# Order of three helpers' work in a macaron decoder kernel: the attention's levels, the normed blocks, the last norm's scale

## The chip, the cores and the metric

The kernel runs on one core of a Trainium2 chip. The metric is the device time of one launch in microseconds: 1767.38 us, the median of three runs (1766.87 to 1767.44). The engines are named as the profile does: PE (TensorE's matmuls; PEld its weight loads), DVE (VectorE), ACT (ScalarE), POOL (GpSimd) and SP (the queue that loads weights).

## The reference

Two layers of a decoder over 512 tokens of width 1024. The first mixes tokens by gated linear attention (4 heads), the second by stick-breaking attention (16 heads); each mixer stands between two half-step SwiGLU feed-forward blocks, and a last RMSNorm ends the trunk. All of it is in float32.

```python
def swiglu(h, w_gate, w_up, w_down):
    return (jax.nn.silu(h @ w_gate) * (h @ w_up)) @ w_down

for i in range(DEPTH):                     # DEPTH = 2
    x = x + 0.5 * swiglu(rmsnorm(x, ffn1_norm[i]), ...)
    h = rmsnorm(x, mix_norm[i])
    y = gla_mixer(h, ...) if i % 2 == 0 else sb_mixer(h, ...)
    x = x + y
    x = x + 0.5 * swiglu(rmsnorm(x, ffn2_norm[i]), ...)
return rmsnorm(x, final_norm)
```

Inside the linear attention, with `b` the running sum of the log decay of a chunk:

```python
o_inter = einsum('bhtk,bhkv->bhtv', q_t * exp(b_t), state)
scores  = einsum('bhtk,bhtsk,bhsk->bhts', q_t, exp(b_t - b_s) (causal), k_t)
o_intra = einsum('bhts,bhsv->bhtv', scores, v_t)
k_dec   = k_t * exp(b_last - b_t)
state   = exp(b_last) * state + einsum('bhsk,bhsv->bhkv', k_dec, v_t)
```

## The kernel before

The activations stay on the chip as eight tiles `x0` to `x7` of 128 features by 512 tokens. The kernel runs six phases one after the other: FFN1, the linear attention (GLA), FFN2, FFN3, the stick-breaking attention and FFN4. Weights come in from memory in chunks; each operand of a matmul is split into a high part, rounded to the matmul's short form (`wh` by a cast on ACT, L151), and a low part, what the rounding left (`wl` by a subtraction on DVE, L152). A product is then three matmuls (`mm3`): high by high, low weight by high, high weight by low. The activations are split in the same way (`nh` and `nl` for normed blocks, `xh` and `xl` for ones that are only scaled by the norm's weights, `sh` and `sl` for the summed squares). The feed is a list of entries, one weight tile each; starting an entry issues the casts of up to three entries ahead, and `wh` and `wl` have four buffers each.

The order on each engine is the program's order unless a scope changes it. `tc.high_priority(n)` lets what is issued inside it go ahead of other work that is ready; `ahead()` is that scope with a large n. `tc.issue_after(ins)` puts what is issued inside it behind one named instruction. Each engine then works through its list in order, and an instruction that waits holds up all that is behind it on its engine.

The places that matter here:

- `feat` (L217 on) multiplies all eight blocks of the activations (`st["h"]`, `st["l"]`) with one weight tile of 128 features. It takes the blocks in the order 0 to 7. In an FFN the first entries run on the scaled blocks, and the norm's root is applied after the matmul; meanwhile `normed_input` makes normed blocks (`xn` L878, `nh` L884, `nl` L885) in pairs: 0 and 4, 1 and 5, 2 and 6, 3 and 7. After that the entries use them, and only the scaled ones' results are still multiplied by the root `R`.
- `sums_wide` (L602 on) sums the squares over the features for FFN2, FFN3 and FFN4: it casts the sum `ss` (`sh`, ACT, L605), subtracts (`sl`, DVE, L607) and sends both through TensorE against ones, into `ps_R`. `rstd_wide` makes `R` of that on DVE and ACT (L617 to L625). `two_halves` interleaves two entries of the feed and calls `sums_wide` between them, to be issued behind the fourth-last matmul recorded so far.
- GLA works head by head. `levels` builds a chunk's causal scores by seven block sizes; for each, `prepare` makes a tile `e`: two subtractions of decays (L1168, L1169, DVE), an exponential on ACT, and two products with k and q (L1171, L1172, DVE). The score matmuls read `e` into a bank `ps_S`, and DVE picks each level's share out of it (L1187, L1211), which frees the bank. `output` makes the decayed keys `kd` (L1237, an exponential, L1244), transposes them on TensorE (`ps_kd`, L1255), updates the state (L1275, L1277) and norms the head's output (L1296 to L1321). `evac_q`, `evac_k`, `evac_v` and `evac_g` empty the matmul banks of q, k, v and the output gate (`gn`, L1070); the output gate then goes on with `sg` and `gn` (L1076, L1080). Between these steps the feed's matmuls run.
- `to_tokens` (L1632 on) turns the x tiles to token rows at the end of FFN4, after the last updates of x (L365). It loads the last norm's weights as `fin` and multiplies them by a constant on DVE (L1649), put behind the last of ACT's copies of the turned tiles; `last` reads `fin`.

Of the kernel before, what the change touches and what calls it, by code (L numbers as in the profile page):

```python
# [18 lines left out]
P = 128  # L19
# [27 lines left out]
def decoder(ctx: ExitStack, tc: tile.TileContext, a: dict, out: bass.AP):  # L47
# [284 lines left out]
    def down(w, r0, nf, hs, part, nxt, late=0, homes=()):  # L332
# [7 lines left out]
        def body(W):  # L340
# [13 lines left out]
            for m in range(nd):  # L354
# [3 lines left out]
                if m < len(homes):  # L358
# [242 lines left out]
    def sums_wide(pool, after):  # L601

        ss = st["ss"]
        h = sp.tile([P, T], F32R, tag="sq", name="sh")
        nc.scalar.copy(h, ss)  # L605
        l = pool.tile([P, T], F32R, tag="t", name="sl")
        nc.vector.tensor_tensor(out=l, in0=ss, in1=h.bitcast(F32), op=ALU.subtract)  # L607
# [19 lines left out]
    def two_halves(between=None):  # L627
# [28 lines left out]
    class FFN:  # L656
# [328 lines left out]
        def run(self, between=None):  # L985
            with tc.tile_pool(name="hp", bufs=8, reuse_waits="tile") as self.hp, tc.tile_pool(
# [34 lines left out]
    class GLA:  # L1021
# [25 lines left out]

        def evac_q(self, h, ps):
            self.q[h] = self.page("q")
            nc.vector.scalar_tensor_tensor(  # L1050
                out=pair(self.q[h]),
                in0=flat(ps),
                scalar=float(P) ** -0.5,
                in1=pair(st["R"]),
                op0=ALU.mult,
                op1=ALU.mult,
            )

        def evac_k(self, h, ps):
            self.k[h] = self.page("k")  # L1060
            nc.vector.tensor_tensor(out=pair(self.k[h]), in0=flat(ps), in1=pair(st["R"]), op=ALU.mult)

        def evac_v(self, c, i, ps):
            nc.scalar.activation(
                pair(self.v[i][:, c * 256 : c * 256 + 256]), flat(ps), AF.Copy, scale=st["r4"][:, i : i + 1]
            )

        def evac_g(self, j, ps):
            self.gn[j] = self.gp.tile([P, T], F32, tag="g", name="gn")
            nc.vector.tensor_tensor(out=pair(self.gn[j]), in0=flat(ps), in1=pair(st["R"]), op=ALU.mult)  # L1070
# [82 lines left out]
        def levels(self, h):  # L1153
# [6 lines left out]
            def prepare(B):  # L1160
# [10 lines left out]
                nc.vector.tensor_tensor(out=e0, in0=e0, in1=halves(k)[0], op=ALU.mult)  # L1171
                nc.vector.tensor_tensor(out=e1, in0=e1, in1=halves(q)[1], op=ALU.mult)  # L1172
                return e

            def seconds(t, B):
# [55 lines left out]
        def output(self, h):  # L1231
# [5 lines left out]
            nc.vector.tensor_tensor(  # L1237
                out=kd[:, 0:n3].rearrange("p (n s) -> p n s", n=3),
                in0=bl[:, 0:3].to_broadcast([P, 3, P]),
                in1=b[:, 0:n3].rearrange("p (n s) -> p n s", n=3),  # L1240
                op=ALU.subtract,
            )
            act(kd[:, 0:n3], kd[:, 0:n3], AF.Exp)
            nc.vector.tensor_tensor(out=kd[:, 0:n3], in0=kd[:, 0:n3], in1=k[:, 0:n3], op=ALU.mult)  # L1244
# [388 lines left out]
    def to_tokens(tp):  # L1633
# [3 lines left out]
        for hf in range(2):  # L1637
# [5 lines left out]
                    )  # L1643
            for i in range(NT):
                xt[i, hf] = xs[hf * 4 + i]
                copied = nc.scalar.copy(xt[i, hf], ps[i]).ins

        with tc.issue_after(copied):
            nc.vector.tensor_scalar(out=fin, in0=fin, scalar1=2.0 * float(D) ** 0.5, scalar2=None, op0=ALU.mult)  # L1649

    def last(dh, i, ps, c0, c1):
# [336 lines left out]
```

## Time and profile before

| what | value |
| --- | --- |
| median of three runs | 1767.38 us (1766.87 to 1767.44) |
| profiled execution | 1767.14 us, of which the span from first to last instruction is 1765.2 us |
| DVE busy | 1506.7 us (85%) |
| ACT busy | 1063.3 us (60%) |
| TensorE's granted clock | 0.999 |
| bytes read | 175.17 MB, 100 GB/s over the span |

In the rows below, a row of the timeline is: start and duration in microseconds, engine, line of the program, operation, output and inputs by the program's names, shapes, number of instructions; in brackets how long the engine was idle ahead of it and what ended that. A matmul's duration contains the time in which it overlaps with the next, so the pace of matmuls is read from one start to the next. The share of busy time is an average: TensorE is busy nearly all the time, and what an edit is worth is read from the places at which TensorE stands.

### The profile page before, as it was taken

The numbers are of one execution on the slowest core, as the hardware profiler recorded it, in microseconds if no ns is written. First come the engines' busy times: TensorE is split into PE (matmuls) and PEld (weight loads), VectorE is DVE, ScalarE is ACT, GpSimd is POOL, SyncE is SP. The second block draws the span as 40 slices with busy tenths as digits, with TensorE's granted clock in tenths as the row PEclk, the third lists the DMA queues.
The fourth block names the chain that finished last, engine by engine and source line by source line (L and its number), as shares of the span: only waits on it lengthen the run. The fifth ranks groups of instructions, "written<-read, shape, count | busy, mean of one in ns | idle before, by whom it ended". The sixth has DMA issues, their size and how long they took to land.

```text
span 1765.2 us, 31380 instructions
## 1 busy us (share of the span) xinstructions
PE 1751.6 (99%) x12714; PEld 1630.2 (92%) x12714; DVE 1506.7 (85%) x2490; ACT 1063.3 (60%) x1899; POOL 55.7 (3%) x77
## 2 busy tenths in 40 slices
PE   9999999999999999999999999999999999999998
PEld 8999999889888899999989999999888889999997
DVE  8999797786888999889799988977898679997986
ACT  7556555554655565555656555656888745555555
POOL 0000000200000000000000000010000000000000
PEclk9999999999999999999999999999999999999999
DMA  5543435422123433444434334352212234434341
GB/s 168 155 122 106 136 105 149 113 72 72 50 89 103 125 114 120 120 120 126 133 94 132 106 123 135 102 131 83 84 49 74 70 96 132 132 99 129 110 136 61
DMA packets 186389, 193.14 MB, mean 109 GB/s; under 512 B 4931, under 2 KB 171125, under 8 KB 186245
## 3 DMA queue, kind: packets, MB, share of 16 engines
q1 hardware_dynamic: 177760, 175.91, 31.9%
q0 software_dynamic: 8240, 14.95, 4.6%
q8 instruction: 99, 1.62, 0.4%
q14 instruction: 46, 0.37, 0.1%
q10 hardware_dynamic: 244, 0.29, 0.0%
HBM read 175.17 MB, written 2.10 MB: 100 GB/s over the span
## 4 chain that ended last, share of the span: by engine, by line
PE 86%; DVE 9%; ACT 3%; issue 1%; DMA 1%; SPq 0%; DVEq 0%; ACTq 0%
PE ps_w L776 22%; PE ps_d L80 15%; PE ps_q L776 11%; PE ps_f L80 10%; PE ps_z L776 5%; PE ps_w L410 5%; PE ps_t L80 4%; PE ps_b L80 3%; PE ps_q L410 2%; DVE wl L152 1%; PE ps_z L410 1%; PE ps_z L1476 1%; PE ps_oT L1561 1%; DVE xn L878 1%; PE ps_bt L80 1%
## 5 line engine op out<-in xcount | busy, mean ns | idle before, releaser
L152 DVE TENSOR_TENSOR wl<-raw,wh 128x1024 fp32r<-128x1024 f32 x241 | 255.1, 1059 | 40.7 <-ACT wh L151 40.0
L151 ACT CAST wh<-raw 128x1024 fp32r<-128x1024 f32 x241 | 222.2, 923 | 71.5 <-PE ps_f L80 25.4
L152 DVE TENSOR_TENSOR wl<-s,wh 128x1024 fp32r<-128x1024 f32 x160 | 195.2, 1220 | 64.5 <-ACT wh L151 64.0
L776 PE MATMUL ps_w<-th,wh 128*128 128x256 f32 x864 | 239.0, 277 | 0.2
L776 PE MATMUL ps_w<-th,wl 128*128 128x256 f32 x864 | 237.7, 275 | 1.2 <-DVE wl L152 1.2
L776 PE MATMUL ps_w<-tl,wh 128*128 128x256 f32 x864 | 237.6, 275 | 0.0
L151 ACT CAST wh<-s 128x1024 fp32r<-128x1024 f32 x160 | 168.6, 1054 | 6.0 <-DVE s L762 6.0
L776 PEld LDWEIGHTS ps_w<-th,wh 128*128 128x128 f32 x864 | 165.8, 192 | 1.4 <-ACT o L813 1.1
L776 PEld LDWEIGHTS ps_w<-th,wl 128*128 128x128 f32 x864 | 165.8, 192 | 1.4 <-DVE wl L152 1.4
L80 PE MATMUL ps_f<-xh,wh 128*128 128x512 f32 x432 | 166.4, 386 | 0.0
L776 PEld LDWEIGHTS ps_w<-tl,wh 128*128 128x128 f32 x864 | 165.9, 192 | 0.0
L80 PE MATMUL ps_f<-xh,wl 128*128 128x512 f32 x432 | 164.2, 380 | 0.5 <-DVE wl L152 0.5
L80 PE MATMUL ps_f<-xl,wh 128*128 128x512 f32 x432 | 163.9, 379 | 0.0
L80 PE MATMUL ps_d<-hh,wh 128*128 128x512 f32 x416 | 157.8, 379 | 0.0
L80 PE MATMUL ps_d<-hh,wl 128*128 128x512 f32 x416 | 157.7, 379 | 0.0
L80 PE MATMUL ps_d<-hl,wh 128*128 128x512 f32 x416 | 157.7, 379 | 0.0
L152 DVE TENSOR_TENSOR wl<-rawd,wh 128x1024 fp32r<-128x1024 f32 (+1 forms) x100 | 94.8, 961 | 8.0 <-ACT wh L151 8.0
L804 ACT COPY ps_z<-ps_w 128x256 f32<-128x256 f32 x72 | 26.0, 362 | 118.1 <-PE ps_w L776 117.9
L361 POOL DMA_DIRECT2D x<-d x53 | 46.0, 913 | 1555.0 <-ACT d L360 1097.4
L80 PEld LDWEIGHTS ps_f<-xl,wh 128*128 128x128 f32 x432 | 81.7, 189 | 11.6
L80 PEld LDWEIGHTS ps_f<-xh,wl 128*128 128x128 f32 x432 | 81.7, 189 | 11.4 <-DVE wl L152 0.9
L80 PEld LDWEIGHTS ps_f<-xh,wh 128*128 128x128 f32 x432 | 81.7, 189 | 10.8
(357 smaller groups left out, 5426.0 us busy)
## 6 DMA issues: line engine op xcount, KB each, us to landing
raw<-in_ffn_w_gate_dram SPq DMA_DIRECT2D x43, 1024.0 KB, 5.4
raw<-in_ffn_w_up_dram SPq DMA_DIRECT2D x43, 1024.0 KB, 5.4
rawd<-in_ffn_w_down_dram SPq DMA_DIRECT2D x84, 512.0 KB, 3.9
x<-d POOLq DMA_DIRECT2D x53, 256.0 KB, 4.6
raw<-in_gla_w_in_dram SPq DMA_DIRECT2D x12, 1024.0 KB, 5.3
raw<-in_sb_w_in_dram SPq DMA_DIRECT2D x16, 512.0 KB, 3.7
raw<-in_gla_w_out_dram SPq DMA_DIRECT2D x4, 1024.0 KB, 5.6
raw<-in_sb_w_in_dram SPq DMA_DIRECT2D x4, 1024.0 KB, 5.1
```

Of the source, the lines that this page charges most:

```text
L80: st["pe"] = nc.tensor.matmul(ps, l, r, start=first, stop=last).ins
L151: nc.scalar.copy(h[:, k], part)
L152: nc.vector.tensor_tensor(out=l[:, k], in0=part, in1=h[:, k].bitcast(F32), op=ALU.subtract)
L361: nc.gpsimd.dma_start(xs[k], d, accum_op=ALU.add)
L410: st["pe"] = nc.tensor.matmul(ps, l_, r_, start=first and c + n == 0, stop=c == 1 and n == 2, skip_group_check=True).ins
L776: st["pe"] = nc.tensor.matmul(o, l_, r_, start=first and j + n == 0, stop=j == 3 and n == 2, skip_group_check=True).ins
L804: v["copied"] = nc.scalar.copy(z, w).ins
L878: nc.vector.scalar_tensor_tensor(out=t, in0=xs[k], scalar=g, in1=st["R"], op0=ALU.mult, op1=ALU.mult)
L1476: nc.tensor.matmul(o_, l_, r_, start=first, stop=last, skip_group_check=True)
L1561: nc.tensor.matmul(po[e * 64 : e * 64 + 64, j * P : T], self.v[j][:, c : c + 64], self.wt[p, e][bk][:, c0 : c0 + n], start=j == 0, stop=j ...
```

## The change

Four edits; no instruction is added or removed, and the lists of POOL and SP stay as they are.

1. `feat` takes the blocks in the order `st["made"]`. That is 0 to 7 at a phase's start, and 0, 4, 1, 5, 2, 6, 3, 7 once the normed blocks are used.
2. `sums_wide` gets two instructions: the high part's matmul is issued behind the fourth-last matmul recorded, as before, the low part's behind the last one.
3. In GLA the evacuations of q, k, v and the gate, all of `prepare`, and `kd` are issued inside `ahead()`.
4. The last norm's scaling is issued behind the last update of x instead of behind ACT's last copy.

```diff
-                for k in part:
-                    mm3(ps, wh[:, k], wl[:, k], st["h"][k], st["l"][k], k == 0, k == KD - 1)
+                for i in part:
+                    k = st["made"][i]
+                    mm3(ps, wh[:, k], wl[:, k], st["h"][k], st["l"][k], i == 0, i == KD - 1)
...
-                nc.vector.scalar_tensor_tensor(
+                st["updated"] = nc.vector.scalar_tensor_tensor(
                     out=x, in0=flat(ps), scalar=0.5, in1=x, op0=ALU.mult, op1=ALU.add
-                )
+                ).ins
...
-        with tc.high_priority(100), tc.issue_after(after):
-            mm(ps, ones_r, turns(h), True, False)
-            mm(ps, ones_r, turns(l), False, True)
+        for r, ins, first in ((h, after[0], True), (l, after[1], False)):
+            with tc.high_priority(100), tc.issue_after(ins):
+                mm(ps, ones_r, turns(r), first, not first)
...
-                    between(recent[-4])
+                    between((recent[-4], recent[-1]))
...
-        st["h"], st["l"] = st["nh"], st["nl"]
+        st["h"], st["l"], st["made"] = st["nh"], st["nl"], range(KD)
...
                 st["h"], st["l"] = zip(*self.n)
+                st["made"] = [k for j in range(4) for k in (j, j + 4)]
...
         def evac_k(self, h, ps):
             self.k[h] = self.page("k")
-            nc.vector.tensor_tensor(out=pair(self.k[h]), in0=flat(ps), in1=pair(st["R"]), op=ALU.mult)
+            with ahead():
+                nc.vector.tensor_tensor(out=pair(self.k[h]), in0=flat(ps), in1=pair(st["R"]), op=ALU.mult)
...
-                nc.vector.tensor_tensor(out=e0, in0=ref, in1=b0, op=ALU.subtract)
-                nc.vector.tensor_tensor(out=e1, in0=b1, in1=ref, op=ALU.subtract)
-                act(e, e, AF.Exp)
-                nc.vector.tensor_tensor(out=e0, in0=e0, in1=halves(k)[0], op=ALU.mult)
-                nc.vector.tensor_tensor(out=e1, in0=e1, in1=halves(q)[1], op=ALU.mult)
+                with ahead():
+                    nc.vector.tensor_tensor(out=e0, in0=ref, in1=b0, op=ALU.subtract)
+                    nc.vector.tensor_tensor(out=e1, in0=b1, in1=ref, op=ALU.subtract)
+                    act(e, e, AF.Exp)
+                    nc.vector.tensor_tensor(out=e0, in0=e0, in1=halves(k)[0], op=ALU.mult)
+                    nc.vector.tensor_tensor(out=e1, in0=e1, in1=halves(q)[1], op=ALU.mult)
...
-                copied = nc.scalar.copy(xt[i, hf], ps[i]).ins
-
-        with tc.issue_after(copied):
+                nc.scalar.copy(xt[i, hf], ps[i])
+
+        with tc.issue_after(st["updated"]):
             nc.vector.tensor_scalar(out=fin, in0=fin, scalar1=2.0 * float(D) ** 0.5, scalar2=None, op0=ALU.mult)
```

`evac_q`, `evac_v`, the first operation of `evac_g` and the three operations of `kd` are put inside `ahead()` in the same way.

Three places show how the engines' lists change. The line numbers of the changed kernel are up to eight higher than those of the kernel before.

The first is DVE in FFN4, before, around the last norm's scaling:

```order
L365 SCALAR_TENSOR_TENSOR x_84<-ps_d,x_84 128x512
L1649 TENSOR_SCALAR fin<-fin 128x1024
L152 TENSOR_TENSOR wl<-s_19889,wh 128x1024
L152 TENSOR_TENSOR wl<-raw,wh 128x512
L152 TENSOR_TENSOR wl<-s_19937,wh 128x1024
```

and in the changed kernel, where it stands now:

```order
L366 SCALAR_TENSOR_TENSOR x_87<-ps_d,x_87 128x512
L366 SCALAR_TENSOR_TENSOR x_88<-ps_d,x_88 128x512
L1657 TENSOR_SCALAR fin<-fin 128x1024
L152 TENSOR_TENSOR wl<-raw,wh 128x1024
L1664 SCALAR_TENSOR_TENSOR x_81<-ps_bt,x_81 128x512
```

The scaling went from ahead of four weights' low parts, past some twenty operations, to just ahead of the program's last `wl`.

The second is PE in FFN2, at the first entry that uses normed blocks (`nh_6466`, `nh_6470` are blocks 0 and 4, `nh_6515`, `nh_6519` blocks 1 and 5, `nh_6570` block 2 and `nh_6621` block 3). Before:

```order
L80 MATMUL ps_f_6680<-nh_6466,wl_6584 128x512
L80 MATMUL ps_f_6680<-nl_6467,wh_6583 128x512
L80 MATMUL ps_f_6680<-nh_6515,wh_6583 128x512
L80 MATMUL ps_f_6680<-nh_6515,wl_6584 128x512
L80 MATMUL ps_f_6680<-nl_6516,wh_6583 128x512
L80 MATMUL ps_f_6680<-nh_6570,wh_6583 128x512
L80 MATMUL ps_f_6680<-nh_6570,wl_6584 128x512
L80 MATMUL ps_f_6680<-nl_6571,wh_6583 128x512
L80 MATMUL ps_f_6680<-nh_6621,wh_6583 128x512
L80 MATMUL ps_f_6680<-nh_6621,wl_6584 128x512
L80 MATMUL ps_f_6680<-nl_6622,wh_6583 128x512
```

and in the changed kernel:

```order
L80 MATMUL ps_f_6680<-nh_6466,wl_6584 128x512
L80 MATMUL ps_f_6680<-nl_6467,wh_6583 128x512
L80 MATMUL ps_f_6680<-nh_6470,wh_6583 128x512
L80 MATMUL ps_f_6680<-nh_6470,wl_6584 128x512
L80 MATMUL ps_f_6680<-nl_6471,wh_6583 128x512
L80 MATMUL ps_f_6680<-nh_6515,wh_6583 128x512
L80 MATMUL ps_f_6680<-nh_6515,wl_6584 128x512
L80 MATMUL ps_f_6680<-nl_6516,wh_6583 128x512
L80 MATMUL ps_f_6680<-nh_6519,wh_6583 128x512
L80 MATMUL ps_f_6680<-nh_6519,wl_6584 128x512
```

Block 4 now stands second and block 3 seventh, as they are made. The lists of DVE and ACT hardly change here, except that a pair's two casts and two subtractions now stand next to each other for blocks 3 and 7.

The third is DVE in GLA, about the stretch in which the fourth head's levels are made (`e`) and weights' low parts (`wl_5614`) go between. Before:

```order
L152 TENSOR_TENSOR wl_5614<-raw_5198,wh_5613 128x1024
L1168 TENSOR_TENSOR e_5664<-b_4642 128x32x8
L1169 TENSOR_TENSOR e_5664<-b_4642 128x32x8
L1076 SCALAR_TENSOR_TENSOR sg_5600<-gn_5598,sg_5600 128x512
L1211 TENSOR_TENSOR S_5546<-ps_S_5634,ident_73 64x4x64 x2
L1171 TENSOR_TENSOR e_5664<-e_5664,k_4628 128x32x8
L1172 TENSOR_TENSOR e_5664<-e_5664,q_4506 128x32x8
L1080 TENSOR_TENSOR gn_5598<-gn_5598,sg_5600 128x512
L1187 COPY_PREDICATED S_5546<-lvl_4156,ps_S_5635 128x8x32
```

and in the changed kernel (its L1175, L1176 are the subtractions and L1178, L1179 the products of `e`):

```order
L1175 TENSOR_TENSOR e_5760<-b_4642 128x128x2
L1176 TENSOR_TENSOR e_5760<-b_4642 128x128x2
L1175 TENSOR_TENSOR e_5794<-b_4642 128x256
L1178 TENSOR_TENSOR e_5712<-e_5712,k_4628 128x64x4
L1179 TENSOR_TENSOR e_5712<-e_5712,q_4506 128x64x4
L1178 TENSOR_TENSOR e_5760<-e_5760,k_4628 128x128x2
L1179 TENSOR_TENSOR e_5760<-e_5760,q_4506 128x128x2
L1176 TENSOR_TENSOR e_5794<-b_4642 128x256
L1076 TENSOR_TENSOR gn_5693<-ps_f_5621,R_4263 128x512
L1341 TENSOR_TENSOR ol_5526<-on_5108,oh_5525 128x512
L1178 TENSOR_TENSOR e_5794<-e_5794,k_4628 128x256
L1179 TENSOR_TENSOR e_5794<-e_5794,q_4506 128x256
```

All levels of the head, `e_5712` to `e_5794` among them, now stand ahead of `wl_5614` and of the picks (L1187, L1211) that free the score banks; before, they were spread behind it.

More of the change, by code (lines that the diff above doesn't have):

```diff
@@ L1049, in evac_q @@
             self.q[h] = self.page("q")
[L1050 to L1057, printed above, removed]
+            with ahead():
+                nc.vector.scalar_tensor_tensor(
+                    out=pair(self.q[h]),
+                    in0=flat(ps),
+                    scalar=float(P) ** -0.5,
+                    in1=pair(st["R"]),
+                    op0=ALU.mult,
+                    op1=ALU.mult,
+                )
         def evac_k(self, h, ps):
             self.k[h] = self.page("k")
-            nc.vector.tensor_tensor(out=pair(self.k[h]), in0=flat(ps), in1=pair(st["R"]), op=ALU.mult)
+            with ahead():
+                nc.vector.tensor_tensor(out=pair(self.k[h]), in0=flat(ps), in1=pair(st["R"]), op=ALU.mult)
         def evac_v(self, c, i, ps):
-            nc.scalar.activation(
-                pair(self.v[i][:, c * 256 : c * 256 + 256]), flat(ps), AF.Copy, scale=st["r4"][:, i : i + 1]
-            )
+            with ahead():
+                nc.scalar.activation(
+                    pair(self.v[i][:, c * 256 : c * 256 + 256]), flat(ps), AF.Copy, scale=st["r4"][:, i : i + 1]
+                )
         def evac_g(self, j, ps):
             self.gn[j] = self.gp.tile([P, T], F32, tag="g", name="gn")
-            nc.vector.tensor_tensor(out=pair(self.gn[j]), in0=flat(ps), in1=pair(st["R"]), op=ALU.mult)
+            with ahead():
+                nc.vector.tensor_tensor(out=pair(self.gn[j]), in0=flat(ps), in1=pair(st["R"]), op=ALU.mult)
             s = self.ep.tile([P, T], F32, tag="s", bufs=2, name="sg")
@@ L1167, in prepare @@
                 ref = b0[:, :, B - 1 : B].to_broadcast([P, T // (2 * B), B])
[L1168 to L1172 removed]
+                with ahead():
+                    nc.vector.tensor_tensor(out=e0, in0=ref, in1=b0, op=ALU.subtract)
[3 more added lines that the diff above has]
+                    nc.vector.tensor_tensor(out=e1, in0=e1, in1=halves(q)[1], op=ALU.mult)
                 return e
@@ L1236, in output @@
             kd = ep.tile([P, T], F32, tag="e", name="kd")
[L1237 to L1244, printed above, removed]
+            with ahead():
+                nc.vector.tensor_tensor(
+                    out=kd[:, 0:n3].rearrange("p (n s) -> p n s", n=3),
+                    in0=bl[:, 0:3].to_broadcast([P, 3, P]),
+                    in1=b[:, 0:n3].rearrange("p (n s) -> p n s", n=3),
+                    op=ALU.subtract,
+                )
+                act(kd[:, 0:n3], kd[:, 0:n3], AF.Exp)
+                nc.vector.tensor_tensor(out=kd[:, 0:n3], in0=kd[:, 0:n3], in1=k[:, 0:n3], op=ALU.mult)
             eb = hp.tile([P, T], F32, tag="eb", name="eb")
```

## The prediction

> **What bounds the kernel now.** I read the page's busy shares first, then the view of TensorE's waits, then the timelines around each of them.
>
> ```profile
> PE 1751.6 (99%) x12714; PEld 1630.2 (92%) x12714; DVE 1506.7 (85%) x2490; ACT 1063.3 (60%) x1899; POOL 55.7 (3%) x77
> ```
>
> ```profile
> core 0 of [0], span 1765.2 us
> PE ps_w L776 <- DVE wl L152: 1.2, 1, 1.2
> PE ps_f L80 <- DVE nl L885: 0.8, 3, 0.3
> PE ps_S L80 <- DVE e L1172: 0.6, 2, 0.4
> PE ps_kd L1255 <- DVE kd L1244: 0.3, 1, 0.3
> PE ps_R L80 <- DVE sl L607: 0.2, 1, 0.2
> PE ps_b L80 <- DVE wl L152: 0.2, 1, 0.2
> ```
>
> TensorE is busy for 1751.6 of 1765.2 us, so an edit that removes no matmul has 13.6 us to win at the very most, start and end of the program included. The second view (engine, line, releaser: total, times, longest) says where a releaser is known. The five rows ahead of the last are the places that the change speaks of, 3.1 us together; the last one lies in the gated linear attention's tail. The question is which of these waits really ends, and what is late next behind it. This is an accounting of a few microseconds: 0.2% of the time, about what a measurement of this kernel tells from no change, is 3.5 us.
>
> **Last norm's scaling.** The largest single wait is near the end. ACT, PE and DVE rows of the timeline (start, duration, operation, idle before it):
>
> ```profile
> 1710.38 1.05 ACT L151 CAST wh<-s 128x1024 fp32r<-128x1024 f32 x1
> 1713.82 0.28 PE L776 MATMUL ps_z<-nl,wh 128*128 128x256 f32 x1
> 1713.93 0.28 PE L776 MATMUL ps_w<-th,wh 128*128 128x256 f32 x1
> 1713.49 0.69 DVE L1649 TENSOR_SCALAR fin<-fin 128x1024 f32<-128x1024 f32 x1 [4.02 <-DMA fin<-in_final_norm_dram]
> 1714.10 1.22 DVE L152 TENSOR_TENSOR wl<-s,wh 128x1024 fp32r<-128x1024 f32 x1
> 1715.37 0.38 PE L776 MATMUL ps_w<-th,wl 128*128 128x256 f32 x1 [1.16 <-DVE wl L152]
> 1735.29 1.23 DVE L152 TENSOR_TENSOR wl<-raw,wh 128x1024 fp32r<-128x1024 f32 x1 [0.30 <-ACT wh L151]
> 1740.30 0.69 DVE L1656 SCALAR_TENSOR_TENSOR x<-ps_bt,x 128x512 f32<-128x512 f32 x1 [3.78 <-PE ps_bt L80]
> ```
>
> VectorE stands 4.02 us at the scaling, whose operand is still on its way from memory. Queued behind it is the low part of a weight (wl), and TensorE waits for that: 1.44 us from 1713.93 to 1715.37, where its neighbour took 0.11. The change puts the scaling behind the last update of x. Then nothing but the cast on ACT holds wl: it is done at 1710.38 + 1.05 = 1711.43, wl would be done at about 1711.43 + 1.22 = 1712.65, and TensorE needs it at 1714.04. The wait goes wholly: 1.44 - 0.11 = 1.33 us. **I take 1.3.** The same VectorE queue also gets the three weights behind it earlier, so none of these is the next wait. In its new place the scaling costs 0.69 us of VectorE just ahead of the wl of 1735.29, into which 0.30 us of idle time falls; wl ends up to 0.4 later. That weight is for the last of the four token entries, and VectorE idles 3.78 us before 1740.30, so there is cover; without it the price would be 0.4. Ends of this term: 0.9 to 1.4.
>
> **Order of the normed blocks.** Blocks are made in pairs 0,4,1,5,2,6,3,7 and were used 0 to 7, so block 3 was wanted fourth and made seventh.
>
> ```profile
> 587.24 0.38 PE L80 MATMUL ps_f<-nh,wl 128*128 128x512 f32 x1
> 587.87 0.48 PE L80 MATMUL ps_f<-nl,wh 128*128 128x512 f32 x1 [0.25 <-DVE nl L885]
> 589.35 1.22 DVE L152 TENSOR_TENSOR wl<-raw,wh 128x1024 fp32r<-128x1024 f32 x1
> 591.00 0.38 PE L80 MATMUL ps_f<-nh,wl 128*128 128x512 f32 x1
> 1437.51 0.38 PE L80 MATMUL ps_f<-xl,wh 128*128 128x512 f32 x1
> 1437.73 0.38 PE L80 MATMUL ps_R<-sh,one_r 128*128 128x512 f32 x1
> 1438.23 0.48 PE L80 MATMUL ps_R<-sl,one_r 128*128 128x512 f32 x1
> 1438.55 0.38 PE L80 MATMUL ps_f<-xh,wh 128*128 128x512 f32 x1
> ```
>
> A 128x512 matmul without a wait starts 0.22 us after the one before it (1437.51 to 1437.73), and the one behind a late one 0.32 after it (1438.23 to 1438.55), so a wait costs 0.10 more than its own length. At 587.87 the loss is 0.63 - 0.22 + 0.10 = 0.51 us. The view counts three such waits, one in each later FFN: 1.5 in all. With blocks used as made, block 3 stands seventh and the wait is gone. What is late next is wl of the following entry: it ends at 589.35 + 1.22 = 590.57 and is first read at 591.00, a slack of 0.43 against the 0.51 gained. So between 0.3 and 0.5 is kept in each. In the first FFN the slack is smaller still:
>
> ```profile
> 47.65 1.22 DVE L152 TENSOR_TENSOR wl<-raw,wh 128x1024 fp32r<-128x1024 f32 x1
> 49.08 0.38 PE L80 MATMUL ps_f<-nh,wl 128*128 128x512 f32 x1
> ```
>
> 48.87 against 49.08 caps the gain there at 0.2; I take 0.1.
>
> **Low part of the summed squares.** It was issued right behind the high part and now comes three matmuls (0.65 us) later, which covers its subtraction.
>
> ```profile
> 560.06 0.48 PE L80 MATMUL ps_R<-sh,one_r 128*128 128x512 f32 x1
> 560.79 0.48 PE L80 MATMUL ps_R<-sl,one_r 128*128 128x512 f32 x1 [0.24 <-DVE sl L607]
> 561.31 0.69 DVE L617 TENSOR_SCALAR v<-ps_R 128x512 f32<-128x512 f32 x1 [0.57 <-PE ps_R L80]
> 561.95 1.05 ACT L151 CAST wh<-raw 128x1024 fp32r<-128x1024 f32 x1 [1.94 <-PE ps_f L80]
> 562.90 0.63 ACT L653 ACTIVATE R<-v 128x512 f32<-128x512 f32 x1
> ```
>
> FFN2 lost 560.79 - 560.06 - 0.22 = 0.51 at the low part (the 0.10 behind it is owed to the high part's own wait), FFN4 by the rows above 0.50 - 0.22 + 0.10 = 0.38, FFN3 nothing that the waits show. Against it stands that the root R now starts from a later matmul. But R's first ACT step (562.90) did not wait for v, done at 562.00; it stood behind ACT's cast, which waited for TensorE to finish an entry. The three matmuls that the cast waits for now stand ahead of the low part, so the cast comes about 0.7 earlier and v, by 0.52 behind a low part at about 561.0, ends at 562.2: R starts some 0.5 earlier in FFN2, as much as TensorE gains. So R's chain, and with it the wl of 589.35, keeps its slack. FFN2 then gives 0.51 + 0.3 = 0.8, FFN4 0.38 + 0.3 = 0.7, FFN3 0.5. **With the first FFN, 2.1 us for both edits.** Ends: 1.0, if wl takes back most of what the blocks gain, and 2.6, if all is kept.
>
> **Priority in the linear attention.** Levels, decayed keys and the evacuations of q, k, v, g go ahead of other work. The two waits for e and the one for kd, with what VectorE does:
>
> ```profile
> 435.94 0.28 PE L80 MATMUL ps_S<-e 128*64 128x64 f32 x2 [0.26 <-DVE e L1172]
> 462.18 0.69 DVE L1070 TENSOR_TENSOR gn<-ps_f,R 128x512 f32<-128x512 f32 x1 [2.13 <-PE ps_f L80]
> 489.37 0.69 PE L80 MATMUL ps_S<-e 128*64 128x64 f32 x16 [0.36 <-DVE e L1172]
> 505.24 0.55 DVE L1244 TENSOR_TENSOR kd<-kd,k 128x384 f32<-128x384 f32 x1
> 505.94 0.52 PE L1255 MATMUL ps_kd<-ident,kd 128*128 128x128 f32 x3 [0.31 <-DVE kd L1244]
> ```
>
> ```profile
> 472.00:490.00 18.00, 17.64 (x140) 14.69 (x135) 17.92 (x36) 11.84 (x20) 0.00 (x0) 1.00 0.19 60
> 490.00:506.00 16.00, 15.69 (x100) 13.62 (x99) 16.00 (x28) 12.07 (x21) 0.00 (x0) 1.00 0.29 96
> ```
>
> The windows' columns are the stretch, its length, and busy time on PE, PE's loads, DVE, ACT, POOL. Between 462.18 and 506 VectorE has next to no idle time, and the change gives it the same work in another order. Thus e can come early and the waits of 435.94 and 489.37 end (0.26 + 0.36, with 0.10 each for the restart 0.8), but kd of 505.24 has about the same work ahead of it as before, counted from the gn of 462.18, which TensorE releases. Of what TensorE gains up to 505, only what moves that release is kept: about 0.4, from the first wait. Behind kd, VectorE has room again, and the tail's wait of 0.2 + 0.10 for wl ends, since that wl now goes ahead of one operation. **I take 0.7.** Ends: a gain of 2.2, if kd's wait (0.31 + 0.10) goes too and the score matmuls that were issued in several pieces among others run in one; a loss of 1.0, since what is put behind the levels (weights' low parts, picks that empty the score banks) can itself be late once: a low part that comes one of its own durations late is 1.2.
>
> As a rule of the Trainium skill (Perfetto Trace Analysis, "Optimizing Scalar/DVE Operations"), a saturated VectorE is helped by fewer and larger operations; this edit only reorders them. By that rule the attention would give 0 and the sum 3.4, and the trace agrees in so far as the 16.00 of 16 us are without a gap.
>
> **Sum.** 1.3 + 2.1 + 0.7 = 4.1 us. The profiled execution took 1767.14, of which 1765.2 span and 1.9 around it; the median of the runs is 0.24 above it. So 1767.38 - 4.1 = **1763.3 us**. All lower ends together (0.9 + 1.0 - 1.0) give 1766.5, all upper ones (1.4 + 2.6 + 2.2) 1761.2.
>
> **Rivals.**
> 1. *The next wait takes half of it.* In the FFNs wl is late by what the blocks gain (1.0 instead of 2.1), and in the attention kd stays put (0 to 0.4): 1.3 + 1.0 + 0.2 = 2.5, 1764.9 us. For it speak the slack of 0.43 against 0.51 and the 16.00 of 16; against it that R's chain moves forward with TensorE.
> 2. *The attention keeps all it can.* 1.3 + 2.1 + 2.2 = 5.6, 1761.8 us. That needs kd itself earlier, against a full VectorE.
> 3. *VectorE stands in front of exponentials: slower.* Each level subtracts on VectorE, exponentiates on ACT and multiplies on VectorE:
>
> ```profile
> L1171 DVE TENSOR_TENSOR e<-e,k 128x256 f32<-128x256 f32 x16 | 6.9, 433 | 0.1
> ```
>
> Today 16 such multiplications find VectorE idle for 0.1 us in all, because other work lies between. Packed closely, each could stand behind half of a weight's cast on ACT (1.05 / 2 = 0.53): 16 x 0.53 = 8.4 us on an engine that is full, against 4.1 gained: 1767.38 + 4.3 = 1771.7. From 0.26 per multiplication on, the change is slower than before. Against it: in the new order two to four other VectorE operations still stand between most subtractions and their multiplication.
>
> **Chances.** Forecast 0.43 (its own range 1762.4 to 1764.2), rival 1 0.30, rival 2 0.15, rival 3 0.12. The range goes from rival 2's lower side, 1761.0, to the lower ends' sum with rival 3's mild half, 1767.0. Faster by over 0.2% (below 1763.8) takes in rival 2 and most of the forecast: 0.52; within 0.2% rival 1, the rest of the forecast and a mild rival 3: 0.39; slower 0.09.
>
> **What would show it.** Scaling right: no wait of ps_w for wl near 1714, and fin's row without idle time just ahead of the last wl. Blocks right: no wait of ps_f for nl in three FFNs; wrong by its size: a wait of ps_f for wl some 3 us behind that place. Low part right: the two ps_R matmuls three apart and R's first ACT step earlier, not later. Attention right: no wait for e, kd's wait still there; rival 2: that gone too; rival 3: idle time ahead of L1171's successor with ACT's e as the releaser. The forecast is wrong if the span between the end of FFN1 and the start of FFN2 gets longer.

## The result, and the profile after

| kernel | median of the runs | ratio to the kernel before |
| --- | --- | --- |
| before | 1767.47 us (1766.87 to 1769.01, 22 runs) | |
| changed | 1764.66 us (1763.99 to 1766.76, 22 runs) | 0.9985, 95% interval 0.9979 to 0.9991 |

The change makes the kernel 2.8 us faster, 0.15%, clear of no change by the interval. 4.1 were forecast, and with 0.15% the outcome is the one that the prediction calls "within 0.2%" (chance 0.39), not "faster by over 0.2%" (0.52). One run of the experiments below, of the kernel with the evacuations put ahead, took 1795.12 us at a granted clock of 0.948 and is left out. The rows that bear on the change, from the view of TensorE's waits in the profiled execution of the changed kernel (1765.20 us):

```profile
core 0 of [0], span 1763.1 us
PE ps_f L80 <- DVE wl L152: 1.0, 2, 0.5
PE ps_w L777 <- DVE wl L152: 1.0, 1, 1.0
PE ps_o L80 <- DVE st L1285: 0.8, 1, 0.8
PE ps_o L80 <- DVE st L1283: 0.5, 1, 0.5
PE ps_on L80 <- DVE sl L1309: 0.2, 1, 0.2
PE ps_kd L1263 <- DVE kd L1252: 0.2, 1, 0.2
```

The waits for nl, for the squares' sl, for e and for the wl behind fin are gone. New are two waits for the state st, a second wait for wl into ps_f (0.49 us at 48.94, in FFN1), and one for wl into ps_w, which looks like the old one but lies elsewhere. The next rows show where (PE, then DVE):

```profile
1713.26 0.28 PE L777 MATMUL ps_w<-th,wh 128*128 128x256 f32 x1
1713.38 0.28 PE L777 MATMUL ps_w<-th,wl 128*128 128x256 f32 x1
745.92 0.38 PE L777 MATMUL ps_w<-th,wl 128*128 128x256 f32 x1 [0.97 <-DVE wl L152]
743.31 0.69 DVE L762 TENSOR_TENSOR s<-raw 128x512 f32<-128x512 f32 x1 [1.31 <-DMA raw<-in_ffn_w_gate_dram]
```

Behind the old place of fin the matmuls now follow each other at 0.12 us. The wait of 0.97 is in FFN2: a weight came late from memory, and DVE stood 1.31 us for it. The kernel before has no such stop there. The view of the transfers has this load in the changed kernel (the last number is the time from issue to landing in us), and then in the changed kernel without the attention's priority, which is an experiment below:

```profile
raw<-in_ffn_w_gate_dram SPq DMA_DIRECT2D x1, 1024.0 KB, 7.5
```

```profile
raw<-in_ffn_w_gate_dram SPq DMA_DIRECT2D x1, 1024.0 KB, 5.5
```

It is late in more than one execution. In the three profiled kernels that have all four edits (the changed one and two experiments on top of it) this load took 7.5, 6.6 and 8.1 us; in the eleven others it took 5.3 to 5.5. What makes it late was not tried.

To see where the time came from, the same matmul is looked up in both traces (us from the span's start):

| point | before | changed | difference | gained in the stretch |
| --- | --- | --- | --- | --- |
| GLA's single gate matmul into ps_z | 357.45 | 357.55 | +0.10 | FFN1: -0.10 |
| the matmul ahead of the next point (ps_f, xl by wh), FFN2 | 559.71 | 559.79 | +0.08 | GLA: 0.02 |
| first ps_R matmul, FFN2 | 560.06 | 560.31 | +0.25 | this matmul's own wait for sh: -0.17 (with GLA -0.15) |
| a ps_w matmul (th by wh) behind the blocks, FFN2 | 627.76 | 627.05 | -0.71 | sums and blocks, FFN2: 0.96 |
| first ps_R matmul, FFN3 | 882.51 | 882.92 | +0.41 | rest of FFN2, late load in it: -1.12 |
| the same ps_w, FFN3 | 949.60 | 949.57 | -0.03 | blocks, FFN3: 0.44 |
| first ps_R matmul, FFN4 | 1437.73 | 1437.86 | +0.13 | rest of FFN3, attention: -0.16 |
| ps_w, th by wh, ahead of fin's place | 1713.93 | 1713.26 | -0.67 | sums and blocks, FFN4: 0.80 |
| ps_w, th by wl, behind it | 1715.37 | 1713.38 | -1.99 | last norm's scaling: 1.32 |
| end of the span | 1765.2 | 1763.1 | -2.1 | |

The matmul into ps_z and the first ps_R matmul of FFN2 are the **marks** of the experiments: 202.61 us lie between them before, 202.76 in the changed kernel. The second mark has a flaw. It reads sh, ACT's cast of the summed squares, and can be late for it:

```profile
559.71 0.38 PE L80 MATMUL ps_f<-xl,wh 128*128 128x512 f32 x1
560.06 0.48 PE L80 MATMUL ps_R<-sh,one_r 128*128 128x512 f32 x1
559.79 0.38 PE L80 MATMUL ps_f<-xl,wh 128*128 128x512 f32 x1
560.31 0.48 PE L80 MATMUL ps_R<-sh,one_r 128*128 128x512 f32 x1
```

The first two rows are of the kernel before, the others of the changed one. Without a wait the second start would be 0.22 behind the first; it is 0.35 and 0.52. So the difference of 0.15 lies at the mark itself, and up to the matmul ahead of it the two kernels take 202.26 and 202.24. The six profiled kernels whose attention has no priority at all lie between 202.39 and 202.61 by the marks, and between 202.17 and 202.26 up to that matmul. The tables below give both.

### The profile page after: what moved, and what is told of

It is laid out like the page before. It is cut to its first block, busy times and chain, and to the rows that moved or that the text cites. A ratio compares the mean times of both kernels' runs of the same rounds, so it can differ in the third digit from the quotient of the medians.

```text
span 1763.1 us, 31372 instructions
## 1 busy us (share of the span) xinstructions
PE 1749.9 (99%) x12714; PEld 1630.6 (92%) x12714; DVE 1506.9 (85%) x2490; ACT 1064.1 (60%) x1899; POOL 55.6 (3%) x77
## 4 chain that ended last, share of the span: by engine, by line
PE 85%; DVE 9%; ACT 3%; DMA 2%; issue 1%; DVEq 0%; SPq 0%; ACTq 0%
PE ps_w L777 20%; PE ps_d L80 15%; PE ps_f L80 14%; PE ps_q L777 10%; PE ps_t L80 5%; PE ps_z L777 5%; PE ps_w L411 4%; PE ps_b L80 3%; DVE wl L152 2%; PE ps_q L411 2%; DMA raw<-in_ffn_w_gate_dram 1%; PE ps_z L1484 1%; PE ps_z L411 1%; PE ps_oT L1569 1%; PE ps_bt L80 1%
```

## The experiments

Three questions were open: what the attention's priority is worth and why, whether the two edits in the FFNs work as the prediction has it, and what could be kept beyond them. Theory A for the attention is that VectorE is full between the gn of 462 and kd of 505, so that putting some of its work ahead only changes what TensorE waits for.

### Without the attention's priority, and with it alone

The first kernel undoes edit 3 (all `with ahead()` in GLA), the second makes edit 3 alone.

> The changed kernel with the attention's priority undone, the other three edits kept. Marks: the single gate matmul into ps_z near 357.5 and the first ps_R matmul of FFN2 near 560; between them lie 202.61 us before and 202.76 in the changed kernel. Theory A (VectorE is full from the gn of 462 to kd of 505, so the edit only exchanges TensorE's waits for e against waits for st): 202.6 between the marks, the waits for e back (0.6 in all), those for st gone, time 1764.5, no different from the changed kernel. Rival B (the edit is worth 0.7 and something else took that back): 203.3 between the marks and 1765.4.

> The kernel before with the attention's priority alone. Theory A: 202.7 to 202.8 between the marks (202.61 before), kd's product ends at 505.8 as before, waits for st of 1.3 in all, time within 0.2 us of the kernel before plus 0.1. Rival B: 0.7 less between the marks and in the time.

| kernel | median | ratio to before | between the marks | to the matmul ahead of the second mark |
| --- | --- | --- | --- | --- |
| without the priority | 1763.75 us (10 runs) | 0.9979 (0.9969 to 0.9988) | 202.39 | 202.18 |
| the priority alone | 1767.95 us (10 runs) | 1.0004 (0.9995 to 1.0014) | 202.62 | 202.19 |

Both of TensorE's views have the waits where theory A puts them. Without the priority:

```profile
PE ps_S L80 <- DVE e L1174: 0.6, 2, 0.3
PE ps_kd L1257 <- DVE kd L1246: 0.3, 1, 0.3
```

and with the priority alone:

```profile
PE ps_o L80 <- DVE st L1283: 0.8, 1, 0.8
PE ps_o L80 <- DVE st L1281: 0.5, 1, 0.5
PE ps_kd L1261 <- DVE kd L1250: 0.2, 1, 0.2
```

The priority gains nothing: 0.6 us of waits for e become 1.3 us of waits for st. By the marks it costs 0.0 (alone) to 0.37 (202.76 against 202.39, on top of the other edits), but of the 0.37, 0.30 is the second mark's wait for sh. Up to the matmul ahead of it the priority changes 202.26 to 202.19 and 202.18 to 202.24: nothing that these traces resolve, in either direction. Rival B, which had 203.3 and 1765.4 without the priority, falls. By the medians the change without the priority is 0.9 us faster than the change, though the intervals overlap; the attention's rows do not account for that.

The rows of DVE at both ends of the stretch, in the kernel changed, and its window beside that of the kernel before (length, then busy time of PE, PE's loads, DVE, ACT, POOL):

```profile
461.80 0.69 DVE L1076 TENSOR_TENSOR gn<-ps_f,R 128x512 f32<-128x512 f32 x1 [2.14 <-PE ps_f L80]
505.26 0.56 DVE L1252 TENSOR_TENSOR kd<-kd,k 128x384 f32<-128x384 f32 x1
461.50:505.80 44.30, 42.81 (x310) 36.68 (x308) 43.88 (x83) 31.98 (x54) 0.00 (x0) 1.00 0.21 72
```

```profile
461.50:505.80 44.30, 43.73 (x311) 37.20 (x310) 43.54 (x84) 32.36 (x55) 0.00 (x0) 1.00 0.18 57
```

VectorE's stretch starts 0.38 earlier (461.80 for 462.18), as the wait of 435.94 gives, and yet kd starts at 505.26 for 505.24: the 0.38 is used up on the way, and TensorE, which comes to st early, waits there.

### The state put ahead too

```diff
+                with ahead():
                     if i == 0:
                         nc.vector.tensor_copy(s, o)
                     else:
                         nc.vector.scalar_tensor_tensor(out=s, in0=sts[-1], ...)
```

> The changed kernel with the state's updates (the copy and the two multiply-adds of st) put ahead too. Theory A: the waits for st (0.8 + 0.5) go, and TensorE stands as much longer at kd, whose product still ends near 505.8; between the marks 202.6 to 202.9, time 1764.6. Rival B (the place of st in VectorE's queue is what took the gain): the 1.3 us are won, 201.4 between the marks, time 1763.3.

1766.11 us (1763.49 to 1769.05, 10 runs), ratio 0.9993 (0.9984 to 1.0002); 204.11 us between the marks, 1.35 more than in the changed kernel. Neither theory had this. The waits for st go, and kd is no wait either: its place in the list moved as well, and its product starts at 503.61. What comes in their place is ACT's cast of a head's squares:

```profile
499.77 0.48 PE L80 MATMUL ps_on<-sh,one 128*128 128x512 f32 x1 [2.09 <-ACT sh L1309]
498.34 0.73 DVE L1305 TENSOR_TENSOR osq<-osq 128x512 f32<-128x512 f32 x1
499.10 0.62 ACT L1309 CAST sh<-osq 128x512 fp32r<-128x512 f32 x1 [0.53 <-DVE osq L1305]
```

The cast waits for the sum osq on VectorE, and that stands behind what was put ahead. The wait of 2.09 has a tail that the views of waits do not show. From 501.51 on, TensorE's matmuls start 0.43 apart instead of 0.22, up to 504.50:

```profile
501.94 0.63 PE L80 MATMUL ps_f<-xl,wh 128*128 128x512 f32 x1
502.37 0.63 PE L80 MATMUL ps_f<-xh,wh 128*128 128x512 f32 x1
502.00:505.00 3.00, 3.00 (x9) 2.44 (x8) 3.00 (x6) 2.94 (x7) 0.00 (x0) 0.55 0.09 12
```

The last row is the window's; the figure behind POOL is the clock granted to TensorE, 0.55 here. By the rows from 501.20 to 504.83 this costs about 1.7 us (an estimate: nine starts in 3.63 us where nine at 0.215 take 1.94). Without it some 202.4 would lie between the marks, where theory A had 202.6 to 202.9. So the core of theory A, that a gain at one place is paid at another, fits; its place was wrong, and neither theory had the clock. Over 360 to 560 us the granted clock is 0.99 in three profiled kernels, this one and two below that stop TensorE for over 2 us in the attention, and 1.00 in the eleven others.

### Work taken off VectorE

```diff
-            nc.vector.tensor_tensor(out=self.gn[j], in0=self.gn[j], in1=s, op=ALU.mult)
+            nc.gpsimd.tensor_tensor(out=self.gn[j], in0=self.gn[j], in1=s, op=ALU.mult)
```

> The changed kernel with the output gate's last product (gn times sg, 8 times 0.69 us, 6 of them between gn and kd) on POOL instead of VectorE. Theory A: VectorE's queue from gn to kd gets 3.6 us shorter, the waits for st and kd (1.5 in all) go, 201.0 to 201.5 between the marks, time 1763.2. Rival C (what holds st and kd is not VectorE's amount of work but its order, or the two engines get in each other's way): waits and time stay, or VectorE's other operations get longer and the time rises by 1 or more.

1767.96 us (10 runs), ratio 1.0006 (0.9997 to 1.0015), 206.21 us between the marks: 3.45 more than in the changed kernel, and rival C. The product takes twice as long on POOL as the 0.69 us on VectorE, and the next user waits for it, three times by up to 1.2 us, with all that is behind it. TensorE's longest wait there, 2.65 us in front of 484.74, is for a weight's low part:

```profile
L1086 POOL TENSOR_TENSOR gn<-gn,sg 128x512 f32<-128x512 f32 x8 | 12.0, 1503 | 86.4 <-ACT sg L654 86.4
DVE on L1337 <- POOL gn L1086: 2.7, 3, 1.2
PE ps_f L80 <- DVE wl L152: 2.7, 1, 2.7
482.79 1.90 DVE L152 TENSOR_TENSOR wl<-raw,wh 128x1024 fp32r<-128x1024 f32 x1
```

In the changed kernel this low part starts at 479.93 and takes 1.21 us. Here y and two products for on, which stood behind it, stand ahead of it in VectorE's new list, and it takes 1.90 while a product of POOL runs (482.34 to 483.61). Behind the wait the granted clock is 0.57 from 484 to 488, and the matmuls start 0.43 apart, which by the rows costs about another 1.5 us (estimate). The late load of FFN2 stands in this execution too (8.1 us), but behind the second mark, so the 3.45 do not hold it. Other rows of VectorE are longer as well, sg with a mean of 785 ns for 689 before. So this run does not settle whether less work on VectorE would help: it brought a new dependence, another order on VectorE, longer operations beside POOL's and a lower clock with it.

### Which part of the priority does it

Each of three kernels has the other three edits and one part of edit 3.

> The three other edits with only the decayed keys (kd) put ahead in the attention. Between the marks (single gate matmul into ps_z, first ps_R matmul of FFN2) lie 202.39 us without any priority and 202.76 with all of it. Theory A (VectorE is full there, so a piece put ahead makes another late): 202.2 to 202.6, kd's wait of 0.3 gone or smaller and another wait in its place. Rival (each piece helps by itself, only their sum is too much): kd's wait of 0.43 and its earlier one of 0.16 gone, 201.8.

> The three other edits with only the levels (e) put ahead in the attention. Theory A: the waits for e (0.45 and 0.50 with their restart) go and about as much comes back at st or kd, 202.2 to 202.8 between the marks. Rival: 201.4, the waits for e gone and nothing in their place.

> The three other edits with only the evacuations of q, k, v and the gate put ahead. They free banks that TensorE does not wait for in the profile. Theory A: 202.3 to 202.6 between the marks, waits for e and kd as without priority. Rival (the gate's evacuations, which start the gate's chain early, are what makes st late): waits for st and 202.8 or more.

| part put ahead | median | ratio to before | between the marks (none: 202.39) | to the matmul ahead (none: 202.18) |
| --- | --- | --- | --- | --- |
| decayed keys kd | 1763.00 us (9 runs) | 0.9975 (0.9965 to 0.9985) | 201.95 | 201.71 |
| levels e | 1769.93 us (10 runs) | 1.0015 (1.0006 to 1.0025) | 207.22 | 206.98 |
| evacuations of q, k, v, gate | 1763.76 us (9 runs) | 0.9979 (0.9970 to 0.9989) | 202.85 | 202.23 |

Two of the parts differ in sign. The levels alone are the worst: 4.8 us lost. DVE's and PE's rows there:

```profile
402.06 0.42 DVE L1171 TENSOR_TENSOR e<-b 128x256 f32<-128x256 f32 x1 [5.23 <-PE ps_S L80]
481.50 0.82 PE L1258 MATMUL ps_kd<-ident,kd 128*128 128x128 f32 x3 [3.67 <-DVE kd L1247]
```

VectorE stands 5.23 us in front of a level that it cannot make yet, because TensorE has to finish with an earlier level first (the tiles named e have six buffers, which kd and a head's norm use too). TensorE does not stand there, and the changed kernel has a like stop:

```profile
398.99 0.43 DVE L1175 TENSOR_TENSOR e<-b 128x256 f32<-128x256 f32 x1 [3.86 <-PE ps_S L80]
```

What costs time is kd, which stayed in its old class and fell behind the levels: TensorE waits 3.67 us for it, and behind that wait the granted clock is 0.66 from 481 to 486, some 1.7 us more (estimate: 0.34 of 5.00). With kd alone ahead, its product comes before one weight's low part and two other operations:

```profile
501.63 1.22 DVE L152 TENSOR_TENSOR wl<-raw,wh 128x1024 fp32r<-128x1024 f32 x1
502.77 0.55 DVE L1247 TENSOR_TENSOR kd<-kd,k 128x384 f32<-128x384 f32 x1
503.24 0.68 DVE L1078 SCALAR_TENSOR_TENSOR sg<-gn,sg 128x512 f32<-128x512 f32 x1
504.78 0.49 PE L1258 MATMUL ps_kd<-ident,kd 128*128 128x128 f32 x3
```

It starts at 502.77 for 505.34 in the kernel without any priority, TensorE no longer waits for it, and nothing that was put behind is waited for. The rival had 201.8, theory A 202.2 to 202.6; measured are 201.95. Up to the matmul ahead of the second mark the gain is 0.47, far more than the 0.09 by which kernels with the same attention differ there. So theory A in its strict form falls too: in a full queue the order can still gain, where what is moved is small and urgent and what it passes has slack. The evacuations change nothing up to that matmul (202.23). Their 0.46 lies at the second mark, which starts 0.62 behind the matmul ahead of it, where 0.22 is the pace:

```profile
562.34 0.48 PE L80 MATMUL ps_R<-sh,one_r 128*128 128x512 f32 x1 [0.23 <-ACT sh L606]
```

Whether the evacuations are what makes sh late is not shown.

### The two edits in the FFNs, one at a time

> The kernel before with the order of the normed blocks alone. Theory A (the blocks' gain is capped by wl of the next entry, whose slack of 0.43 is short of 0.51): the three waits for nl go, and in FFN2 to FFN4 the wl of the next entry is waited for by 0.1 to 0.2 each; together 0.3 to 0.5 won in each; in FFN1 a wait for wl of 0.5 in place of those for nl. Rival (the cap does not bind): 0.51 in each, no wait for wl.

> The kernel before with the later low part of the summed squares alone. Theory A (ACT's cast sets when the root starts): low part without a wait, 0.51 won in FFN2, 0.38 in FFN4, 0 in FFN3, and R's first ACT step earlier than before (562.90) by 0.4 to 0.65, FFN3's by 0.1 to 0.2. Rival (the root's chain hangs on the low part): R's first step later by up to 0.4 and later waits for nl longer by as much.

One run each, 1765.86 and 1766.93 us: too few for a time, but the rows tell. With the order of the blocks alone, nl is not waited for, and wl of the next entry is, in FFN2 and by the same amount in FFN3 and FFN4:

```profile
590.30 0.48 PE L80 MATMUL ps_f<-nh,wl 128*128 128x512 f32 x1
590.62 0.38 PE L80 MATMUL ps_f<-nl,wh 128*128 128x512 f32 x1
```

The first of these starts 0.16 us late and the next at 0.32: 0.26 of the 0.51 is given back. That is theory A's cap. With the low part alone, FFN2's rows are:

```profile
561.58 0.42 PE L80 MATMUL ps_R<-sh,one_r 128*128 128x512 f32 x1
562.49 0.38 PE L80 MATMUL ps_R<-sl,one_r 128*128 128x512 f32 x1
562.69 1.05 ACT L151 CAST wh<-raw 128x1024 fp32r<-128x1024 f32 x1 [1.22 <-PE ps_f L80]
562.90 0.69 DVE L617 TENSOR_SCALAR v<-ps_R 128x512 f32<-128x512 f32 x1 [0.71 <-PE ps_R L80]
563.69 0.63 ACT L653 ACTIVATE R<-v 128x512 f32<-128x512 f32 x1
```

R's first step comes 2.11 us behind the high part; in the kernel before it was 562.90 - 560.06 = 2.84. So the root starts 0.73 earlier against TensorE (0.4 to 0.65 were expected) although its sum is finished later. But v now ends at 563.59, 0.10 ahead of R: cast and sum have come about level, and how much later the low part could go was not tried. With both edits together (the changed kernel) the two help each other: the root's lead gives wl its slack back, and of the 0.26 only 0.10 stays.

### The first FFN, and a version with all that helps

In the changed kernel FFN1 waits for wl. Two cures, both on the kernel without the attention's priority: the old order of blocks in FFN1 alone, and the last pair's differences (`ts`, four subtractions on DVE) issued behind the next entry's start:

```diff
-                    st["made"] = [k for j in range(4) for k in (j, j + 4)]
+                if self is not phases[0]:
+                    st["made"] = [k for j in range(4) for k in (j, j + 4)]
```

```diff
-                ts = self.tp.tile([P, 4, H], F32, tag="s", bufs=4, name="ts")
-                sub(ts[:, 0], x[:, H:T], x[:, 0:H])
...
+                def differences():
...
+                if j < 3 or self is not phases[0]:
+                    differences()
+                else:
+                    self.last_pair = differences
...
+                if self is phases[0]:
+                    self.last_pair()
                 todo = self.sums()
```

> The three edits without the attention's priority, the first FFN keeping blocks 0 to 7. Theory: its waits for nl come back (0.60 lost in the kernel before) and the one for wl goes (0.76 lost in the changed kernel): 0.1 to 0.2 less, time 1763.6. Rival: nl and wl waits both, time 1764.3.

> The three edits without the attention's priority, and in the first FFN the last pair's differences ts (four subtractions of 0.42) issued behind the next entry's start, so that its wl comes some 1.1 us earlier. Theory: the wait of 0.49 for wl near 48.9 goes and at most 0.35 comes back as a wait for nl, because wl is then put ahead of the last two nl; 0.3 to 0.7 less than without it, time 1763.2. Rival: the whole is given back at nl or at th, time 1763.75.

1763.46 us (0.9979, 0.9969 to 0.9988) and 1763.25 us (0.9975, 0.9966 to 0.9985), 10 runs each. In the second one wl ends at 46.34 instead of 48.89 and neither wl nor nl is waited for:

```profile
45.12 1.22 DVE L152 TENSOR_TENSOR wl<-raw,wh 128x1024 fp32r<-128x1024 f32 x1
46.25 1.28 DVE L886 TENSOR_TENSOR nl<-xn,nh 128x512 fp32r<-128x512 f32 x2
```

The last run joins this to the priority for kd:

> The three edits, of the attention's priority only that for the decayed keys, and the first FFN's last differences behind the next entry's start. If the two additions do not touch each other: 202.0 us between the marks in the attention, no wait for nl or wl near 49 in the first FFN, time 1762.4 (1763.75 without both; the one alone gave 0.5, the other 0.75). If the first FFN's shift changes what follows: 1763.0 or more.

1763.29 us (1762.49 to 1765.02, 11 runs), ratio 0.9977 (0.9968 to 0.9986). Between the marks lie 202.01 us (201.79 up to the matmul ahead), and no wait is left near 49, as expected; the time is 0.9 above what the two gains add up to. Its fastest run is 1762.49, that of the kernel with kd alone 1762.50: whole runs of one kernel scatter by 1 to 2 us, more than these last gains. A part of that scatter stands in the traces: in three of the fourteen profiled executions (the levels alone, the evacuations alone, the low part alone) the matmuls from 7.3 to 10.3 us start 0.43 apart instead of 0.22, and the first mark comes at 359.2 to 359.5 us, where the others have it at 357.2 to 358.0. What can be said is that six versions without the levels' priority lie at 0.9975 to 0.9979 of the kernel before, below the changed kernel's 0.9985, with intervals that overlap with its own, and that the runs do not rank them.

## Why the prediction was right or wrong

- **Last norm's scaling: right.** 1.3 was forecast and 1.32 measured, 1.42 by the matmul behind it (1715.58 before, 1713.49 now), which has the 0.10 of the restart that this term left out. The new place costs nothing: fin runs at 1732.82 without idle time, and the wl behind it is not waited for.
- **Low part of the squares: right, with its mechanism.** That ACT's cast, and not the sum, set when the root started is what the run with this edit alone shows (0.73 earlier); with the edit the two are about level.
- **Blocks: right in FFN2 to FFN4, wrong in FFN1.** The step that called wl "late next" holds: alone the edit gives back half. With the low part's edit, 0.8 in FFN2, 0.5 in FFN3 and 0.7 in FFN4 were forecast; 0.96, 0.44 and 0.80 measured (FFN2 counted from the first ps_R matmul, which itself is 0.17 later than before). For FFN1 the prediction has: "48.87 against 49.08 caps the gain there at 0.2; I take 0.1". The cap itself was read rightly. wl ends at 48.89, and its first reader starts earlier than before, at 48.94 for 49.08 (the last row is of the changed kernel, the first of the kernel before):

```profile
45.76 0.38 PE L80 MATMUL ps_d<-hh,wh 128*128 128x512 f32 x1
48.94 0.48 PE L80 MATMUL ps_f<-nh,wl 128*128 128x512 f32 x1 [0.49 <-DVE wl L152]
```

  Two things were left out: the 0.10 of the restart behind this wait, and the order of TensorE's own list. In the kernel before, one matmul of the next product (ps_d) stood ahead of that reader, at 45.76; in the changed kernel the first ps_d stands at 54.01, so its 0.22 are now behind the wait instead of ahead of it. TensorE came to wl at about 48.3, waited 0.49 by the view and lost 0.76 by the starts, where the waits for nl had cost 0.60. By the table FFN1 gave -0.1.
- **Attention: wrong.** "I take 0.7" was the mis-sized term; by the marks it is -0.15, within its ends of -1.0 to 2.2, and up to the matmul ahead of the second mark it is 0.02, so nothing was won and the sign is open. The prediction's own sign of being wrong, a longer span between the end of FFN1 and the start of FFN2, came by the marks, though what made the span longer is the mark's wait for sh. The prediction saw that kd would not move, and it did not (505.26 for 505.24). Three steps failed. "Only what moves that release is kept: about 0.4": the release did come 0.38 earlier, but the full queue lost it before kd. And the list of what might be late next named low parts and picks, not the state's updates, which stand between the levels and kd in the same queue. The part of it that TensorE reads next, after the levels that it no longer waits for, is st, and it should have been looked up in the changed list. Third, the tail: its wait for wl (0.21 in front of 529.63) did end, but at 530.68 TensorE starts 0.51 behind the matmul ahead of it, where the pace is 0.22, so the 0.3 that was counted there came back.
- **Rivals.** The outcome lies by rival 1 (1764.9, "the next wait takes half of it") more than by the forecast, but by half of its mechanism: the attention kept nothing, while the FFNs kept nearly all. In the profiled execution another 1.12 went in the rest of FFN2, where the late load stands, so that the median fell so near to rival 1 is partly chance. Rival 3's stall in front of a level was seen in the kernels that put the levels ahead (3.86 us in the changed kernel, 5.23 with the levels alone), though VectorE waits for TensorE there and not for an exponential, and TensorE does not stand meanwhile.
- **The rule on a saturated VectorE** (the Trainium skill, Perfetto Trace Analysis, "Optimizing Scalar/DVE Operations") would, as the prediction reads it, have given 0 for the attention and 3.4 for the rest. The rest gave 3.7 by the medians (1767.47 to 1763.75), and the trace agrees for the edit as made: 43.88 of 44.30 us busy. The 0 is no bound on what an order can do, of which that section says nothing: kd alone gained 0.44 in the same full stretch.
- **What stays open.** By the medians the three other edits gave 3.7 (3.4 forecast), and the priority on top of them -0.9 (0.7 forecast). Of the 0.9 the attention's own rows show 0.06, and 0.37 by the marks. The late load of FFN2 lies behind the marks and fits the rest: it is late in all three executions with all four edits and in none of the eleven others, and TensorE's stop of 0.97 there is of the right size. But with one execution of each kernel, that it is late in most runs is likely and not shown, and why the order in the attention should make it late is open. The prediction had no term for a transfer that moves.

## What to carry to other kernels

When a wait goes, count the slack of the next one from where its consumer will now stand in the changed list, with the restart behind the new wait and with every matmul that changed sides of it. In a full queue, as here, try priority for the single small operation that is waited for before a whole class of work; the class took its buffers along and pushed back what it did not contain. Look at the granted clock behind every long stop: in three kernels here a stop of 2.1 to 3.7 us cost some 1.5 to 1.7 us more than its length. Gains of some tenths of a microsecond are read from the start of the same matmul in both traces, and from one that does not wait itself: the mark used here moved by up to 0.2 between kernels with the same attention, the matmul ahead of it by 0.09.

## What was not expected of the hardware

- Behind the stops of 2.09, 2.65 and 3.67 us in the attention the clock granted to TensorE was 0.55, 0.57 and 0.66 in the windows of 3 to 5 us that follow, and f32 matmuls of 128x512 started 0.43 us apart for 0.22. The stops of at most 0.81 us that the traces of the other kernels show in the attention left it at 1.00 there.
- The same f32 product of 128x512 took 1503 ns on POOL (1.27 to 2.02 us) and 688 on VectorE, and with POOL at work VectorE's sg product took 785 ns in the mean for 689, one low part of a weight 1.90 us for 1.21.
- One and the same load of 1 MB of weights took 6.6 to 8.1 us to land in the three kernels with all four edits and 5.3 to 5.5 in the eleven others, though no edit touches it; in the changed kernel TensorE stood 0.97 us for it. The runs of one kernel spread over 2 us and more.
